# A decoder step on one core: the convolution state turned in another mixer, the sample rows of r finished in a step of their own, one order edge less

## The chip, the core and the metric

The kernel runs on one core of one Trainium2 chip, as one program. The time is device microseconds of that core. Five engines work side by side, each through its own instructions in order: TensorE (PE, with its weight loads shown as PEld), VectorE (DVE), ScalarE (ACT), GpSimd (POOL) and SyncE (SP), which here issues all the DMA transfers. The kernel before takes 2837.52 us (median of three runs, 2835.45 to 2838.09).

## The reference

One step of one layer of a hybrid decoder, in float32, for 2048 prompt tokens and, beside them, for 32 sample tokens (8 requests of 4). Cut to what matters here:

```python
def mixer(xn, s0, lp):
    q, k, v, r, a, u, sv = split_cols(xn @ w_in)
    ...
    o, S = gla_chunked(q, k, v, logg, s0)          # gated linear attention
    o = rmsnorm(o, g_gla_out).reshape(B, T, GLA_WIDTH) * jax.nn.silu(r)
    sv = rmsnorm(jax.nn.gelu(sv).reshape(B, T, SGU_HEADS, SGU_DH), g_sgu)
    z = sgu_spatial(sv, w_s, b_s)                  # mixing of positions in chunks of 128
    s_out = jax.nn.gelu(u) * z.reshape(B, T, SGU_WIDTH)
    return jnp.concatenate([o, s_out], axis=-1) @ w_out, S, sv

def conv_ffn(hn, buf, w_gate, w_up, conv_w, conv_b, w_down):
    g = hn @ w_gate
    gp = jnp.concatenate([buf, g], axis=1)         # buf: the last two rows, state_conv
    c = conv_b + sum(conv_w[j] * gp[:, j:j + T] for j in range(CONV_W))
    return (jax.nn.gelu(c) * (hn @ w_up)) @ w_down, gp[:, -2:]

def layer(x, mk, mv, s0, buf, ...):
    h = x + mixer(rmsnorm(x), s0)
    h = h + mem_attend(rmsnorm(h), mk, mv)         # attention over 256 memory tokens
    return h + conv_ffn(rmsnorm(h), buf)
```

## The kernel before

**Blocks.** The prompt is cut into four blocks of 512 tokens (`s` = 0 to 3). Each block goes through a mixer, the memory attention and the feed-forward network. I call the mixers of the four blocks mixer 1 to mixer 4. The 32 sample tokens ride along: in mixer 2 (`B.mix_sample`, s = 1) as 32 more columns, and in the feed-forward network of block 3 (`B.ffn_sample`, s = 2). In mixer 1, products of the memory's keys and values with weights are folded in between (`qk_steps`, `vo_steps`), whose tiles are `qkp` and `vop`.

**Matmuls.** A float32 product is made of three fast matmuls: each operand is split into a high part (an ACT copy) and a low part (a DVE subtraction); L99, L100 and L101 (`mm3`) are the three products. The splits of weights are L84 and L85. Plain float32 matmuls are used for small things.

**The projection of r.** `tm_steps` makes four steps per projection, each with two of the eight slices of the weight; the tiles `t_wr` collect 128 tokens each. For the sample tokens it works by another way: sixteen "spread" matmuls (L723) put partial sums of the 32 tokens into four groups of 32 rows, ACT copies them out (L727, tile `t_wr1t`), and one matmul with `sum4` (L747) adds the four groups. L887 is the Silu that takes the tiles of r out, four for the prompt's rows and one for the sample rows. The same function serves the projections of v and sv.

**What stands around it in mixer 2.** `mix(h)` (L927 for the prompt, tile `zp`; L935 for the samples, tile `zps`) mixes positions for one of four heads; then DVE (L930, L936), POOL (L940), ACT (`ch`, L84) and POOL again (`cl`) make of it one of the eight inputs `cat` of the output projection. The linear attention runs for two pairs of heads (`p` = 0, 1), each with `diag` (L1006 on POOL, L1009 on PE), seven `level` steps (L1035 to L1061, tiles `e` and `kr`, PE at L1057), `decay` (tiles `kh`, `ktp`, `km`), `states` (`kv`), `chunks` (`op`) and, for the samples, `smp`. Its tail normalizes rows (`onorm`, which reads r at L1187; `gate`, L1192) and turns them back (`back`, `otp`). The output projection `out_proj_steps` (tiles `a_wo`) begins with inputs 4 to 7, those of the mixes. In mixer 2 it has three first steps, `w1`.

**The convolution state.** `sample_conv` loads the sample tokens' convolution state in six pieces of 16 rows (L466, tiles `sc`), transposes it in 22 matmuls into one PSUM tile (L469, `sctp`) and copies that to `sct` (L470). POOL reads `sct` tile by tile for the network of block 3 (L1553), up to eight tiles ahead.

**What sets the order.** The program is a list of steps. `weave` places side lists between the main steps: a triple (steps, first, last) spreads the steps evenly from behind main step `first` to behind main step `last`. In mixer 2 the main steps are sv 0 to 3, a 4, k 5, q 6, v 7 to 10, u 11 and 12, r 13 to 16, then the output projection. Behind step 16 come mixes 3 and 4 and the last four steps of the linear attention; the tail is spread from 16 to 18. `run` loads weights five units ahead of their use. A planner then gives every instruction its place in its engine's order, by the order of the program, by its own model of time and by the buffers that are free: six T buffers (the tiles `e`, `kr`, `pr`, `z`, `sc`, `t_wr1t`, `y` and others), four PSUM banks for sums (`acc`) and four for everything small (`mps`). `behind(first, then)` adds an order edge without a wait: `then` may not stand before `first` on its engine. Two such edges bear on the output projection: in whole projections a matmul of its third row tile stands behind the last `op`; in mixer 2 its very first matmul stands behind the last matmul of the last mix (`B.last_mix`).

Of the kernel before, what the change touches and what calls it, by code (L numbers as in the profile page):

```python
# [12 lines left out]
AF = mybir.ActivationFunctionType  # L13
# [12 lines left out]
NS = 32  # L26
# [7 lines left out]
Q0, K0, V0, R0, A0, U0, SV0 = 0, 256, 512, 1024, 1536, 1552, 2064  # L34
# [3 lines left out]
def hymba_step_kernel(  # L38
# [10 lines left out]
    act, dve, pool, pe = nc.scalar, nc.vector, nc.gpsimd, nc.tensor  # L49
# [23 lines left out]
    def mps(name):  # L73
        return mmp.tile([128, 512], F32, tag="mm", name=name)
# [19 lines left out]
    def behind(first, then):  # L94

        tc.add_manual_dep(then.ins, first.ins.name, in_turn, reason="in turn")
# [270 lines left out]
    for l in range(7):  # L367
# [7 lines left out]
        m = const([128, 256], f"mask{l}", U8)  # L375
# [4 lines left out]
    sum4 = const([128, NS], "sum4")  # L380
# [96 lines left out]
    def weave(main, *sides):  # L477

        out = []
        due = [0.0] * len(sides)  # L480
        at = [0] * len(sides)
        for i, m in enumerate(main):
            out.append(m)
            for j, (steps, first, last) in enumerate(sides):
                if i < first:
                    continue
                due[j] = len(steps) * min(1.0, (i - first + 1) / (last - first + 1))
                while at[j] < len(steps) and at[j] < due[j] - 1e-9:
                    out.append(steps[at[j]])
                    at[j] += 1  # L490
        for j, (steps, _, _) in enumerate(sides):
            out += steps[at[j]:]
        return out
# [216 lines left out]
            return Step(fn, [wmake(w, 4 * j, 4, m0, 256, f"{name}{j}", make, j) for j in range(2)])  # L710
        return Step(fn, [(w, 4 * j, 4, m0, 256, f"{name}{j}") for j in range(2)])

    def tm_steps(w, m0, get_xs, sample, evac, name):


        ps = {}
        held = []

        def spread(j):
            if j == 1:  # L720
                ps["q"] = mps(f"t_{name}q")
            for k, raw in reversed(held):
                pe.matmul(ps["q"][hr[k % 4]], sxg[:, k * NS:(k + 1) * NS], raw, start=j == 1, stop=j == 3)  # L723
            held.clear()
            if j == 3:
                ps["t"] = T_(f"t_{name}t")
                act.activation(ps["t"][:, :512], ps["q"], AF.Copy)  # L727

        def fn(j, wu):
            xs = get_xs()  # L730
            raw, wh, wl = wu
            if sample:
                held.extend((2 * j + kk, raw[:, kk]) for kk in range(2))
                if j % 2:
                    spread(j)
            for c in range(4):
                cs = slice(c * 128, (c + 1) * 128)
                if j == 0:
                    ps[c] = acc(f"t_{name}{c}")
                for kk in range(2):  # L740
                    k = 2 * j + kk
                    mm3(ps[c], xs[k][0][:, cs], xs[k][1][:, cs], wh[:, kk], wl[:, kk], k == 0, k == 7)
                if j == 3:
                    evac(ps[c], c, 128)
            if sample and j == 3:
                ps[4] = mps(f"t_{name}4")
                pe.matmul(ps[4][:NS], sum4, ps["t"][:, :512], start=True, stop=True)  # L747
                evac(ps[4][:NS], 4, NS)

        def unit(j):  # L750
            def load():
                raw = wload(w, 2 * j, 2, m0, 512, f"{name}{j}")
                return raw, *wsplit(raw, f"{name}{j}")
            return load
        return [Step(lambda wu, j=j: fn(j, wu), [unit(j)]) for j in range(4)]

# [84 lines left out]
    def proj_steps(B):  # L843
        s, sample = B.s, B.mix_sample
        T = TM if sample else SB
        nt = 5 if sample else 4
        w = w_in[0]
        xs = lambda: B.xs

        def ev_tm(key, f):  # L850
            def evac(ps, c, n):
                if c == 0:
                    B.__dict__[key] = [U(f"{key}{s}{c}") for c in range(nt)]
                f(B.__dict__[key][c][:n, :512], ps, B.xrs[:n, c:c + 1])
            return evac

        def ev_fm(key, i0, f):
            def evac(mm, ps, c0, cw):
                i = i0 + mm
                if c0 == 0:  # L860
                    B.__dict__.setdefault(key, {})[i] = U(f"{key}{s}{i}")
                f(B.__dict__[key][i][:, c0:c0 + cw], ps, B.xbc[:, c0:c0 + cw])
            return evac

        scaled = lambda o, i, f: dve.tensor_scalar(o, i, f, None, ALU.mult)
        times = lambda o, i, f: dve.tensor_tensor(o, i, f, ALU.mult)

        def gelu_times(o, i, f):
            dve.tensor_tensor(o, i, f, ALU.mult)
            act.activation(o, o, AF.Gelu_apprx_tanh)  # L870

        def a_fn():
            B.aT = T_(f"aT{s}")
            for ci, (c0, cw) in enumerate(chunks_of(sample)):
                ps = mps(f"ap{s}{ci}")
                for k in range(8):
                    pe.matmul(ps[hr[k % 4], :cw], wa[:, k], B.h[k][:, c0:c0 + cw], start=k < 4, stop=k >= 4)
                act.activation(B.aT[:, c0:c0 + cw], ps[:, :cw], AF.Copy)

        out = tm_steps(w, SV0, xs, sample, ev_tm("sv", lambda o, i, f: act.activation(o, i, AF.Gelu_apprx_tanh, scale=f)), f"ws{s}")  # L880
        out.append(Step(a_fn))
        out.append(fm_step(w, K0, xs, sample, ev_fm("k", 0, times), f"wk{s}"))
        out.append(fm_step(w, Q0, xs, sample,
                           ev_fm("q", 0, lambda o, i, f: dve.scalar_tensor_tensor(o, i, 0.125, f, ALU.mult, ALU.mult)), f"wq{s}"))
        out += tm_steps(w, V0, xs, sample, ev_tm("v", scaled), f"wv{s}")
        out += [fm_step(w, U0 + h * 128, xs, sample, ev_fm("u", h, gelu_times), f"wu{s}{h}") for h in (0, 2)]
        out += tm_steps(w, R0, xs, sample, ev_tm("r", lambda o, i, f: act.activation(o, i, AF.Silu, scale=f)), f"wr{s}")  # L887
        return out

    def norm_of(src, ss, c, n):  # L890
# [59 lines left out]
    for p in range(2):  # L950
        t = cp.tile([128, 128], F32, tag=f"S{p}", name=f"Sz{p}", bufs=2)
# [270 lines left out]
    def out_proj_steps(B, unit, src, g, name, sample, first, finished, keep=None, seven=False,  # L1222
                       whole=False):
# [4 lines left out]
        s = B.s  # L1228
# [5 lines left out]
        def half(m2, k0, last, begin=True, end=True):  # L1234

            def fn(wu):
                wh, wl = wu
                x = src()
                if m2 == 0 and last:
                    B.hn, B.sq = [], None  # L1240
                for i in range(2):
                    m = 2 * m2 + i
                    ms = slice(i * 128, (i + 1) * 128)
                    for ci, (c0, cw) in enumerate(chunks_of(sample)):
                        cs = slice(c0, c0 + cw)
                        ps = acc(f"a_{name}{s}{k0}{m}{ci}") if begin else open_.pop(m)
                        for k in range(4):
                            mm = mm3(ps[:, :cw], wh[:, k, ms], wl[:, k, ms], x[k0 + k][0][:, cs], x[k0 + k][1][:, cs],
                                     begin and k == 0, end and k == 3)
                            if name == "wo" and s and not last and k == 0:  # L1250
                                if whole and m == 2:
                                    behind(B.last_o, mm)
                                elif not whole and m == ci == 0:
                                    behind(B.last_mix, mm)
                        if end:
                            dve.tensor_tensor(B.h[m][:, cs], ps[:, :cw], B.h[m][:, cs], ALU.add)
                        else:
                            open_[m] = ps
                    if last:
                        finish(m)  # L1260
            return Step(fn, [unit(k0, m2)])
# [35 lines left out]
        if whole:  # L1297
            out = [half(m2, first, False, end=False) for m2 in (0, 1)]
# [493 lines left out]
    for s, B in enumerate(blocks):  # L1792
# [6 lines left out]
        if B.mix_sample:  # L1799
            def keep():  # L1800
                if not hasattr(smp, "x"):
# [1 line left out]
                return smp.x  # L1803
        w1, w2, stat = out_proj_steps(B, lambda k0, m2, s=s: (w_out[0], k0, 4, m2 * 256, 256, f"wo{s}{k0}{m2}"),
                                      lambda B=B: B.cat, "gx", "wo", B.mix_sample, 4, B.mix_sample, keep, seven=True, whole=not B.mix_sample)
        early = [] if s else [Step(sample_conv)]
        folds = [(qk_steps, 0, 10), (vo_steps, 11, 19)] if s == 0 else []
        steps += weave(proj + w1, *folds, (after, 0, 5), (sgu_st[:1], 6, 6), (early, 9, 9), (sgu_st[1:nst], 11, 11), (sgu_st[nst:nst + 2], 12, 13), (sgu_st[nst + 2:], 16, 16), (gla[:1], 4, 4), (gla[1:2], 6, 6), (gla[2:12], 8, 10), (gla[12:-nlast], 10, 13), (gla[-nlast:], 16, 16), (gtail, 16, 18))
        scales, sc, turns = attention_steps(B)
        x1, x2, xstat = out_proj_steps(B, lambda k0, m2, s=s: wready(vod[k0 // 4][:, m2], f"wx{s}{k0}{m2}"),  # L1810
                                       lambda B=B: B.ao, "gffn", "wx", False, 0, B.ffn_sample, seven=s > 0, whole=True)
# [54 lines left out]
```

## Time and profile before

| | us |
|---|---|
| median of three runs | 2837.52 |
| profiled execution | 2838.75 |
| its span, first to last instruction | 2837.0 |
| PE busy | 2799.4 |
| DVE busy | 1892.2 |
| ACT busy | 1107.4 |
| POOL busy | 567.4 |

The mean granted clock of TensorE over the span is 0.994. How to read the rows: a timeline row gives the start, the time it took, the engine, the source line, the operation, the tile written and the tiles read, the shape and the count of merged instructions; in brackets stands how long the engine was idle before it and whose end it waited for. A row by stages gives, for a stretch of the span, the busy time of each engine with the number of its instructions, then the granted clock as a share of full speed. Matmuls overlap, so the spacing of their starts tells more than the time of one. A DMA row on SP is the issue of a transfer, not the transfer.

### The profile page before, as it was taken

The numbers are of one execution on the slowest core, as the hardware profiler recorded it, in microseconds if no ns is written. First come the engines' busy times: TensorE is split into PE (matmuls) and PEld (weight loads), VectorE is DVE, ScalarE is ACT, GpSimd is POOL, SyncE is SP. The second block draws the span as 40 slices with busy tenths as digits, with TensorE's granted clock in tenths as the row PEclk, the third lists the DMA queues.
The fourth block names the chain that finished last, engine by engine and source line by source line (L and its number), as shares of the span: only waits on it lengthen the run. The fifth ranks groups of instructions, "written<-read, shape, count | busy, mean of one in ns | idle before, by whom it ended". The sixth has DMA issues, their size and how long they took to land.

```text
span 2837.0 us, 47062 instructions
## 1 busy us (share of the span) xinstructions
PE 2799.4 (99%) x17894; PEld 2479.6 (87%) x17894; DVE 1892.2 (67%) x3266; ACT 1107.4 (39%) x1950; POOL 567.4 (20%) x638
## 2 busy tenths in 40 slices
PE   8999999999999999999999999999999999999998
PEld 8887888888887798998888889899999888899997
DVE  6577778777657686655545787666666688665555
ACT  5645545333363444322223545422223545431222
POOL 2002213111101221321321121232221013132222
PEclk9999999999999999999999999999999999999999
DMA  9755579999941236887886225576776324677775
GB/s 310 238 187 193 170 262 340 339 342 329 341 142 62 82 117 233 302 292 276 310 315 232 83 75 177 206 255 247 261 264 230 111 68 135 208 260 270 272 276 185
DMA packets 369687, 638.21 MB, mean 225 GB/s; under 512 B 27370, under 2 KB 238412, under 8 KB 369462
## 3 DMA queue, kind: packets, MB, share of 16 engines
q1 hardware_dynamic: 369462, 635.20, 65.7%
q8 instruction: 142, 2.33, 0.3%
q14 instruction: 83, 0.68, 0.1%
HBM read 507.69 MB, written 127.41 MB: 224 GB/s over the span
## 4 chain that ended last, share of the span: by engine, by line
PE 63%; DVE 3%; ACT 1%; DMA 0%; issue 0%; POOL 0%; DVEq 0%; ACTq 0%
PE d L101 4%; PE d L100 4%; PE d L99 4%; PE a_wx L101 2%; PE a_wx L100 2%; PE a_wx L99 2%; PE s L1057 1%; PE a_wo L99 1%; PE a_wo L100 1%; PE a_wo L101 1%; PE a_wu L99 1%; PE a_wu L100 1%; PE t_wr L99 1%; PE a_wu L101 1%; PE t_wr L100 1%; PE t_wr L101 1%
## 5 line engine op out<-in xcount | busy, mean ns | idle before, releaser
L99 PE MATMUL d<-acth,whi_wd 128*128 128x272 f32 (+1 forms) x688 | 235.3, 342 | 0.0
L100 PE MATMUL d<-actl,whi_wd 128*128 128x272 f32 (+1 forms) x688 | 233.8, 340 | 0.0
L101 PE MATMUL d<-acth,wlo_wd 128*128 128x272 f32 (+1 forms) x688 | 233.4, 340 | 0.0
L1714 DVE TENSOR_TENSOR h<-d,h 128x512 f32<-128x512 f32 (+1 forms) x232 | 133.7, 582 | 148.0 <-PE d L101 148.0
L1607 POOL TENSOR_TENSOR c<-c,bc_f 128x512 f32<-128x512 f32 (+1 forms) x88 | 138.0, 1574 | 135.7 <-ACT c L1606 135.0
L1597 ACT ACTIVATE c<-g,colsb 128x512 f32<-128x512 f32 x88 | 71.8, 816 | 189.4 <-DVE g L1560 142.0
L101 PEld LDWEIGHTS d<-acth,wlo_wd 128*128 128x128 f32 x688 | 129.3, 188 | 15.4 <-issue 1.2
L99 PEld LDWEIGHTS d<-acth,whi_wd 128*128 128x128 f32 x688 | 129.4, 188 | 13.8
L100 PEld LDWEIGHTS d<-actl,whi_wd 128*128 128x128 f32 x688 | 129.4, 188 | 13.7 <-issue 0.4
L1629 POOL TENSOR_TENSOR c<-r_q_wup,c 128x512 f32<-128x512 f32 (+1 forms) x33 | 63.4, 1922 | 332.4 <-DVE r_q_wup L296 212.4
L99 PE MATMUL a_wo<-ch,h_wo 128*128 128x512 f32 (+1 forms) x320 | 112.8, 366 | 2.6 <-ACT ch L88 2.1
L1594 POOL COPY carry<-g 128x2 f32<-128x2 f32 x88 | 29.9, 340 | 423.4 <-DVE g L1560 392.0
L100 PE MATMUL a_wo<-cl,h_wo 128*128 128x512 f32 (+1 forms) x320 | 113.6, 357 | 0.0
L101 PE MATMUL a_wo<-ch,l_wo 128*128 128x512 f32 (+1 forms) x320 | 112.5, 354 | 0.0
L1598 DVE SCALAR_TENSOR_TENSOR c<-g,colsb,c 128x512 f32<-128x512 f32 x88 | 85.4, 971 | 27.8 <-ACT c L1597 27.2
L101 PE MATMUL a_wx<-pTh,wlo_wx 128*128 128x512 f32 x256 | 101.2, 395 | 0.0
L100 PE MATMUL a_wx<-pTl,whi_wx 128*128 128x512 f32 x256 | 100.5, 393 | 0.0
L84 ACT ACTIVATE acth<-c 128x512 fp32r<-128x512 f32 (+1 forms) x88 | 55.9, 637 | 113.5 <-DVE c L1629 80.4
L99 PE MATMUL a_wx<-pTh,whi_wx 128*128 128x512 f32 x256 | 100.1, 394 | 0.0
L1606 ACT ACTIVATE c<-c 128x512 f32<-128x512 f32 (+1 forms) x88 | 56.1, 638 | 89.6 <-DVE c L1599 77.8
L1599 DVE SCALAR_TENSOR_TENSOR c<-g,colsb,c 128x512 f32<-128x512 f32 x88 | 88.4, 1004 | 1.1
L85 DVE TENSOR_TENSOR actl<-c,acth 128x512 fp32r<-128x512 f32 (+1 forms) x88 | 63.1, 719 | 26.7 <-ACT acth L84 25.6
(3753 smaller groups left out, 9731.8 us busy)
## 6 DMA issues: line engine op xcount, KB each, us to landing
whi_wd<-wd SPq DMA_DIRECT2D x66, 512.0 KB, 9.8
wlo_wd<-wd SPq DMA_DIRECT2D x66, 512.0 KB, 9.6
r_wo<-in_w_out_dram SPq DMA_DIRECT2D x32, 512.0 KB, 3.3
wlo_wx<-vod SPq DMA_DIRECT2D x32, 512.0 KB, 4.5
whi_wx<-vod SPq DMA_DIRECT2D x32, 512.0 KB, 4.1
r_wg<-in_w_gate_dram SPq DMA_DIRECT2D x22, 512.0 KB, 5.1
r_wup<-in_w_up_dram SPq DMA_DIRECT2D x22, 512.0 KB, 6.3
r_wd<-in_w_down_dram SPq DMA_DIRECT2D x22, 512.0 KB
```

What stands on the lines that cost most here:

```text
L84: act.activation(hi, src, AF.Copy)
L85: (lo_eng or dve).tensor_tensor(lo, src, hi.bitcast(F32), ALU.subtract)
L99: out = pe.matmul(ps, wh, xh, start=first, stop=False)
L100: pe.matmul(ps, wh, xl, start=False, stop=False)
L101: pe.matmul(ps, wl, xh, start=False, stop=last)
L1597: act.activation(c[:, :SB], g[:, 2:SB + 2], AF.Identity, bias=cb, scale=w2)
L1598: dve.scalar_tensor_tensor(c[:, :SB], g[:, 1:SB + 1], w1, c[:, :SB], ALU.mult, ALU.add)
L1599: dve.scalar_tensor_tensor(c[:, :SB], g[:, 0:SB], w0, c[:, :SB], ALU.mult, ALU.add)
L1606: act.activation(c[:, :T], c[:, :T], AF.Gelu_apprx_tanh)
L1607: pool.tensor_tensor(c[:, :T], c[:, :T], B.fbc[:, :T], ALU.mult)
L1629: (dve, pool)[i].tensor_tensor(c[:, :T], q[i], c[:, :T], ALU.mult)
L1714: dve.tensor_tensor(B.h[m + mm][:, cs], ps[:, :cw], B.h[m + mm][:, cs], ALU.add)
```

## The change

Three edits. First, `tm_steps` gets an argument `apart`. With it, the sum matmul of the sample rows and its Silu leave the fourth step and become a fifth step, `rows`, with an order edge that puts the matmul behind `apart()`. Only the projection of r in mixer 2 uses it, with the last matmul of the last mix. So mixer 2 has one main step more, number 17, and its tail is spread from 17 to 19, as before behind the step with the sample rows. In the program's order, mixes 3 and 4 and the last four steps of the linear attention now stand ahead of the sample rows of r. Second, the edge that put mixer 2's first matmul of the output projection behind the last mix is taken out; the edge of the whole projections stays. Third, `sample_conv` moves from behind main step 9 of mixer 1 to behind main step 1 of mixer 3. What is computed stays the same.

```diff
-    def tm_steps(w, m0, get_xs, sample, evac, name):
+    def tm_steps(w, m0, get_xs, sample, evac, name, apart=None):
...
-            if sample and j == 3:
-                ps[4] = mps(f"t_{name}4")
-                pe.matmul(ps[4][:NS], sum4, ps["t"][:, :512], start=True, stop=True)
-                evac(ps[4][:NS], 4, NS)
+            if sample and j == 3 and not apart:
+                rows()
+
+        def rows():
+            ps[4] = mps(f"t_{name}4")
+            mm = pe.matmul(ps[4][:NS], sum4, ps["t"][:, :512], start=True, stop=True)
+            if apart:
+                behind(apart(), mm)
+            evac(ps[4][:NS], 4, NS)
...
-        return [Step(lambda wu, j=j: fn(j, wu), [unit(j)]) for j in range(4)]
+        out = [Step(lambda wu, j=j: fn(j, wu), [unit(j)]) for j in range(4)]
+        return out + [Step(rows)] if apart else out
...
-        out += tm_steps(w, R0, xs, sample, ev_tm("r", ...), f"wr{s}")
+        out += tm_steps(w, R0, xs, sample, ev_tm("r", ...), f"wr{s}",
+                        (lambda: B.last_mix) if sample else None)
...
-                            if name == "wo" and s and not last and k == 0:
-                                if whole and m == 2:
-                                    behind(B.last_o, mm)
-                                elif not whole and m == ci == 0:
-                                    behind(B.last_mix, mm)
+                            if name == "wo" and s and whole and not last and (m, k) == (2, 0):
+                                behind(B.last_o, mm)
...
-        early = [] if s else [Step(sample_conv)]
+        early = [Step(sample_conv)] if B.ffn_sample else []
...
-        ... (early, 9, 9), ... (gtail, 16, 18))
+        ... (early, 1, 1), ... (gtail, 16 + B.mix_sample, 18 + B.mix_sample))
```

More of the change, by code (lines that the diff above doesn't have):

```diff
@@ L886, in proj_steps @@
         out += [fm_step(w, U0 + h * 128, xs, sample, ev_fm("u", h, gelu_times), f"wu{s}{h}") for h in (0, 2)]
-        out += tm_steps(w, R0, xs, sample, ev_tm("r", lambda o, i, f: act.activation(o, i, AF.Silu, scale=f)), f"wr{s}")
+        out += tm_steps(w, R0, xs, sample, ev_tm("r", lambda o, i, f: act.activation(o, i, AF.Silu, scale=f)), f"wr{s}",
+                        (lambda: B.last_mix) if sample else None)
         return out
@@ L1805, in hymba_step_kernel @@
                                       lambda B=B: B.cat, "gx", "wo", B.mix_sample, 4, B.mix_sample, keep, seven=True, whole=not B.mix_sample)
-        early = [] if s else [Step(sample_conv)]
+        early = [Step(sample_conv)] if B.ffn_sample else []
         folds = [(qk_steps, 0, 10), (vo_steps, 11, 19)] if s == 0 else []
-        steps += weave(proj + w1, *folds, (after, 0, 5), (sgu_st[:1], 6, 6), (early, 9, 9), (sgu_st[1:nst], 11, 11), (sgu_st[nst:nst + 2], 12, 13), (sgu_st[nst + 2:], 16, 16), (gla[:1], 4, 4), (gla[1:2], 6, 6), (gla[2:12], 8, 10), (gla[12:-nlast], 10, 13), (gla[-nlast:], 16, 16), (gtail, 16, 18))
+        steps += weave(proj + w1, *folds, (after, 0, 5), (sgu_st[:1], 6, 6), (early, 1, 1), (sgu_st[1:nst], 11, 11), (sgu_st[nst:nst + 2], 12, 13), (sgu_st[nst + 2:], 16, 16), (gla[:1], 4, 4), (gla[1:2], 6, 6), (gla[2:12], 8, 10), (gla[12:-nlast], 10, 13), (gla[-nlast:], 16, 16), (gtail, 16 + B.mix_sample, 18 + B.mix_sample))
         scales, sc, turns = attention_steps(B)
```

## The prediction

> **What bounds the kernel now.** I read, in this order, the page, the waits of TensorE (PE), PE's busy time and granted clock by stage, and the instruction timelines of PE, ACT, DVE, POOL and SP at the three places the change touches. From the page, then from PE's waits (engine, line, who ended it: us in all, times, longest):
>
> ```profile
> span 2837.0 us, 47062 instructions
> PE 2799.4 (99%) x17894; PEld 2479.6 (87%) x17894; DVE 1892.2 (67%) x3266; ACT 1107.4 (39%) x1950; POOL 567.4 (20%) x638
> ```
>
> ```profile
> PE s L1057 <- DVE kr L1047: 5.0, 2, 3.3
> PE t_wr L747 <- ACT t_wr1t L727: 3.6, 1, 3.6
> ```
>
> PE is busy for 2799.4 of 2837.0 us, so at most 37.6 us of idle time can be won, plus what a low clock costs; taking work from DVE, ACT, POOL or a queue is worth nothing unless PE waits for it. The second wait is that of the matmul which the change moves. The stages (from:to, length, busy us of PE, PEld, DVE, ACT, POOL, granted clock, DMA share, GB/s):
>
> ```profile
> 253.00:266.00 13.00, 10.02 (x32) 8.42 (x33) 8.95 (x16) 2.47 (x5) 1.72 (x1) 0.50 0.24 81
> 972.00:980.00 8.00, 8.00 (x32) 6.43 (x32) 1.66 (x3) 1.34 (x2) 1.34 (x1) 0.57 0.50 187
> 991.00:1011.00 20.00, 18.45 (x146) 16.54 (x146) 19.94 (x45) 5.35 (x7) 7.30 (x5) 0.98 0.27 80
> 1010.00:1017.00 7.00, 6.91 (x29) 6.14 (x30) 2.85 (x7) 2.13 (x5) 0.00 (x0) 0.51 0.67 185
> 1540.00:1560.00 20.00, 20.00 (x93) 16.22 (x92) 7.03 (x11) 7.09 (x12) 1.11 (x2) 1.00 0.48 150
> ```
>
> The first row lies in mixer 1: a stretch at half clock. The next three lie in mixer 2, which has two such stretches; in mixer 3, at 1540, PE is busy throughout at full clock. A microsecond of PE work therefore costs one in mixer 3, while mixers 1 and 2 hold idle time.
>
> **Part 1: sample rows of r, mixer 2.** PE there, with the idle time before an instruction and its releaser in brackets:
>
> ```profile
> 951.87 1.06 PE L927 MATMUL zp<-wsT,sv 128*128 128x128 f32 x8
> 952.86 0.40 PE L935 MATMUL zps<-wss,sv 32*128 32x32 f32 x2
> 953.19 0.50 PE L101 MATMUL t_wr<-h_wr,xl 128*128 128x512 f32 x1
> ...
> 966.43 1.93 PE L723 MATMUL t_wr1q<-r_wr,sxg 128*32 128x512 f32 x16
> 971.91 1.31 PE L747 MATMUL t_wr<-t_wr1t,sum 128*32 128x512 f32 x2 [3.56 <-ACT t_wr1t L727]
> 973.15 2.08 PE L927 MATMUL zp<-wsT,sv 128*128 128x128 f32 x8
> 975.15 0.63 PE L935 MATMUL zps<-wss,sv 32*128 32x32 f32 x2
> 975.72 2.08 PE L927 MATMUL zp<-wsT,sv 128*128 128x128 f32 x8
> ```
>
> ACT, then DVE:
>
> ```profile
> 968.95 2.42 ACT L887 ACTIVATE r<-t_wr,xrs 128x512 f32<-128x512 f32 x4
> 971.24 0.61 ACT L727 ACTIVATE t_wr1t<-t_wr1q 128x512 f32<-128x512 f32 x1
> ...
> 981.77 0.66 ACT L84 ACTIVATE ch<-z 128x544 fp32r<-128x544 f32 x1 [3.50 <-POOL z L940]
> ```
>
> ```profile
> 967.49 2.14 DVE L1105 TENSOR_SCALAR km<-ktps,blk 32x128 f32<-32x128 f32 x8
> 969.56 1.20 DVE L85 TENSOR_TENSOR l_wo<-r_wo,h_wo 128x1024 fp32r<-128x1024 f32 x1
> 975.26 0.75 DVE L930 SCALAR_TENSOR_TENSOR z<-zp,colsb,bsb 128x512 f32<-128x512 f32 x1 [4.50 <-PE zp L927]
> ...
> 1001.84 0.67 DVE L1187 TENSOR_TENSOR o<-o,r 32x512 f32<-32x512 f32 x1
> ```
>
> The spread matmuls end at 968.35 (971.91 − 3.56). Their copy, L727, stands on ACT behind four Silus and ends at 971.85, so L747 keeps PE idle for 3.56 us, and the mixes behind it with it. They need nothing of it. After the wait PE is slow: one mix with its sample part took 2.57 us (973.15 to 975.72), the same instructions 1.32 us before (951.87 to 953.19). From 972 to 980 the clock is 0.57, which loses 8.0 × 0.43 = 3.4 us. The place thus costs 3.56 + 3.4 = 7.0 us.
>
> Changed, the two mixes come first: 2 × 1.32 = 2.6 us at full clock, from 968.35 to 971.0. Their PSUM banks should be there: the last of the copies out of the p=1 transposes (km) ends at 969.63. L747 could then still wait 971.85 − 971.0 = 0.9 us at most, and nothing if matmuls of the output projection stand between; I take 0.4 us. Behind it on PE are only that projection and the state matmuls, work that is there either way. Its Silu moves along; the first reader of row tile 4 of r is L1187 at 1001.84, far behind. So 7.0 − 0.4 = **6.6 us** won, with ends of 7.0 and of about 4 (0.9 us waited, and 2 us of low clock left).
>
> [...]
>
> Does the gain reach the end of mixer 2? From 991 to 1011 DVE is busy 19.94 of 20 us, with norms that start from PE's o tiles. DVE is idle for 4.50 us behind l_wo, waiting for the zp of 973.15; that chain moves with PE, so I let the whole of it slide forward and the thin stretch of 1010 to 1017 with it.
>
> **Part 2: the edge.** Before, the projection's first matmul stands behind the last mix on PE; after, only L747 does. I cost this at nothing: every matmul freed is work that PE does anyway. What it costs if the planner uses the freedom badly is rival 3.
>
> **Part 3: the convolution state.** In mixer 1 (PE; DVE; POOL; all loads on SP with their times in ns to issue; PE later; DVE later):
>
> ```profile
> 173.75 0.40 PE L101 MATMUL t_wv<-h_wv,xl 128*128 128x512 f32 x1
> 173.98 0.40 PE L99 MATMUL t_wv<-h_wv,xh 128*128 128x512 f32 x1
> 174.31 1.55 PE L469 MATMUL sctp<-ident,sc 16*128 16x16 f32 x22
> 175.79 0.50 PE L100 MATMUL t_wv<-l_wv,xh 128*128 128x512 f32 x1
> ```
>
> ```profile
> 175.54 0.68 DVE L1035 TENSOR_TENSOR e<-b 128x512 f32<-128x512 f32 x1
> 176.13 0.52 DVE L470 COPY sct<-sctp 128x352 f32<-128x352 f32 x1
> ```
>
> ```profile
> 176.72 1.15 POOL L1553 COPY gs<-sct 128x16 f32<-128x16 f32 x8 [42.50 <-DVE sct L470]
> ```
>
> ```profile
> L466 SPq DMA_DIRECT2D sc<-in_state_conv_dram x6: 389/462/663, 153.7 to 171.6; - x6
> ```
>
> ```profile
> 169.20 1.05 PE L1057 MATMUL s<-kr,e 128*128 128x128 f32 x8
> ...
> 253.33 2.05 PE L1057 MATMUL s<-kr,e 128*128 128x128 f32 x8 [3.31 <-DVE kr L1047]
> ```
>
> ```profile
> 226.84 0.75 DVE L930 SCALAR_TENSOR_TENSOR z<-zp,colsb,bsb 128x512 f32<-128x512 f32 x1 [1.13 <-PE zp L927]
> ```
>
> The 22 transposes put 175.79 − 173.98 = 1.81 us between two matmuls that otherwise follow at 0.23 us: 1.58 us of PE. With them go one DVE copy (0.52 us), six loads on SP (0.39 to 0.66 us each to issue) and eight POOL copies that ran right behind.
>
> In mixer 3 PE has no gap: **+1.58 us**; DVE (7.03 of 20 us) and POOL (1.11) have room. On SP the loads cost at most 6 × 0.66 = 4 us of issue among weight loads that run five units ahead; on POOL the copies stand ahead of the row norms' powers (L316), 1.15 us, and hold these back if the state comes late. Bounds: the row's own 1.55 us, and, if PE reaches the transposes before the loads have landed, a stall like that of Part 1, 7 us more.
>
> In mixer 1 PE comes 1.58 us earlier to its wait at 250.0 (253.33 − 3.31). It gains only if the level chain it waits for comes earlier too. That chain's last leg starts on DVE behind the z of 226.84, which itself waited for PE (1.13 us). So it moves by the same 1.58 us: **−1.58 us**, the two cancel. Bounds: nothing won, if DVE paces the chain further back; or the whole stall gone: 5.0 us of waits for kr and 13.0 × 0.50 = 6.5 us of low clock, 11.5 us.
>
> **Sum.** 0 − 6.6 + 1.6 − 1.6 = −6.6 us. The profiled execution took 2838.75 us (span 2837.0, 1.75 around it): 2832.2. The median of the runs, 2837.52, is 1.2 us below it: **2831 us**.
>
> **Rivals.**
> 1. *Mixer 1 loosens.* The six state tiles share six T buffers with the levels. A level's e was written only at 175.54, right after the first state tiles were read (174.31); the level before had been used by 170.3 (169.20 + 1.05). Without the tiles the chain could be up to 175.54 − 170.3 = 5.3 us ahead, more than the first wait of 3.31 us, so that the clock stays up. Against it: DVE is crowded later, and the chain is released by PE at 226.8. Worth 3.3 to 11.5 us; middle 7.4: 2824 us.
> 2. *The gain is given back.* The norms at 991 to 1011 fill DVE; if something other than PE starts them, PE waits for them longer by what it came earlier, and 1010 to 1017 keeps its low clock. For it: DVE's 19.94 of 20. Against it: DVE's idle time before 991. 2837 us.
> 3. *Slower: PE takes the projection first.* Without the edge its first matmuls, whose inputs come from mixes 1 and 2, can go ahead of the mixes of heads 3 and 4; PE executes in order, then meets the inputs of the last two heads and waits. The way from the last zp (975.72) to its ch (982.43) is 6.7 us at present. If the fill is used up by then, PE idles 6.7 us, loses 3.4 us by the clock, and DVE's norms start later by the 3.0 us of projection put first (four banks, two inputs, three matmuls of 18.45 / 146 = 0.126 us): 13.1 instead of 7.0 us, so 2843.6 us. [...] Against it: the state matmuls (16 kv, then op) still fill.
> 4. *No effect*: the planner may keep L747 where PE waits for ACT (another ACT instruction put ahead of L727), 2837.5 us.
>
> **How the numbers follow.** A measurement of this kernel tells 0.2% (5.7 us) from no change. Forecast 0.48, by itself 2828 to 2835; rival 1 0.22, rival 2 0.12, rival 3 0.13, rival 4 0.05. Of the forecast's chance 0.30 lies beyond 5.7 us (below 2831.8) and 0.18 within. Faster: 0.30 + 0.22 = 0.52. Same: 0.18 + 0.12 + 0.05 = 0.35. Slower: 0.13. The range 2820 to 2840 leaves out the strongest form of rival 1 and rival 3's upper half and beyond, and takes in a late load in mixer 3.
>
> **What would show it.** Right: no idle time before L747 over 1 us; the two zp groups near 968 to 971 at 1.06 us each; clock 1.00 from 966 to 985; 22 transposes of 1.5 us in mixer 3 without a wait; mixer 1's end moved by about 1.6 us. Wrong: PE idle before a_wo or zp in mixer 2 for over 3 us (rival 3), the thin stretch before 1017 grown (rival 2), or the waits for kr at 250 us gone (rival 1) or longer.

## The result, and the profile after

The changed kernel takes 2824.78 us (median of six runs, 2822.55 to 2829.24) where the kernel before took 2838.69 us beside it (six runs, 2835.45 to 2840.13): a ratio of 0.9953, 95% interval 0.9941 to 0.9966, so 9.7 to 16.7 us of 2838.7, middle 13.3. Repeated later (label a_again below): 0.9957, 0.9945 to 0.9968. The forecast was 2831.0 us, its range 2820 to 2840. The whole interval lies beyond the 0.2% that tell from no change; the direction holds, and the gain is twice the 6.6 us forecast.

From the page of the changed kernel, and from its waits of PE (engine, tile, line, who ended the wait: us in all, times, longest), behind two longer ones at the program's start (2.9 and 2.4 us):

```profile
span 2827.5 us, 47048 instructions
PE 2795.2 (99%) x17894; PEld 2475.8 (88%) x17894; DVE 1887.1 (67%) x3266; ACT 1105.9 (39%) x1950; POOL 572.6 (20%) x638
```

```profile
PE otp L1205 <- DVE vol L85: 2.2, 2, 1.3
PE mkt L588 <- DVE mkf L579: 2.0, 1, 2.0
PE ktp L1103 <- POOL kh L1100: 1.8, 1, 1.8
PE a_wk L99 <- ACT sv L886: 1.3, 1, 1.3
```

The two waits that headed the list before, 5.0 us for `kr` and 3.6 us for `t_wr1t`, are gone. PE idles 2827.5 − 2795.2 = 32.3 us instead of 37.6. The rest of the 9.5 us between the two profiled spans (the changed kernel's profile is of its slowest run, 2829.24 us) is clock: adding up length × (1 − granted clock) over the whole span in 283 equal stretches gives 17.4 us lost before and 11.3 us after. 5.3 + 6.1 = 11.4 us, less 1.9 us by which PE's work itself came out longer.

Mixer 2, PE of the changed kernel (start, time, engine, line, tiles, shape, count):

```profile
960.62 1.92 PE L723 MATMUL t_wr1q<-r_wr,sxg 128*32 128x512 f32 x16
962.48 1.16 PE L934 MATMUL zp<-wsT,sv 128*128 128x128 f32 x8
...
963.90 0.39 PE L99 MATMUL a_wo<-ch,h_wo 128*128 128x272 f32 x1
...
966.25 1.06 PE L934 MATMUL zp<-wsT,sv 128*128 128x128 f32 x8
...
968.40 1.09 PE L1122 MATMUL kv<-v,kt 128*64 128x128 f32 x16
...
980.43 1.02 PE L750 MATMUL t_wr<-t_wr1t,sum 128*32 128x512 f32 x2
```

The mixes follow the spread matmuls at once. Matmuls of the output projection (`a_wo`) already stand between the two mixes, which the edge forbade before. The sum matmul (now L750) starts 980.43 − 966.03 = 14.4 us after ACT has ended the copy that it reads (L727, 965.41 to 966.03) and waits for nothing.

Mixer 1, PE of the kernel before (its `s` of 253.33, with the wait of 3.31 us, stands in the prediction), then of the changed kernel:

```profile
237.77 1.05 PE L1057 MATMUL s<-kr,e 128*128 128x128 f32 x8
...
245.97 1.06 PE L927 MATMUL zp<-wsT,sv 128*128 128x128 f32 x8
...
257.11 2.05 PE L1057 MATMUL s<-kr,e 128*128 128x128 f32 x8 [1.73 <-DVE kr L1047]
260.08 1.11 PE L1096 MATMUL ktp<-ident,kh 128*128 128x128 f32 x4 [0.93 <-POOL kh L1093]
```

```profile
172.14 1.05 PE L1064 MATMUL s<-kr,e 128*128 128x128 f32 x8
...
233.80 1.05 PE L1064 MATMUL s<-kr,e 128*128 128x128 f32 x8
...
242.24 1.06 PE L934 MATMUL zp<-wsT,sv 128*128 128x128 f32 x8
251.04 1.05 PE L1064 MATMUL s<-kr,e 128*128 128x128 f32 x8
252.42 1.13 PE L1064 MATMUL s<-kr,e 128*128 128x128 f32 x8 [0.33 <-ACT h_wof L84]
255.38 1.11 PE L1103 MATMUL ktp<-ident,kh 128*128 128x128 f32 x4 [1.83 <-POOL kh L1100]
```

The level matmuls (`s`, 237.77 to 233.80) and the mix (`zp`, 245.97 to 242.24) stand 3.97 and 3.73 us earlier, not 1.58. The true shift is larger still: the profiled execution of the changed kernel was 2.94 us behind when it came here (the `s` at 169.20 in the prediction stands at 172.14), so counted from that `s` it is 6.91 and 6.67 us. Before, 253.33 − 245.97 − 3.31 = 4.05 us of PE work lay between `zp` and the next `s`, and then PE waited. After, 251.04 − 242.24 = 8.80 us of work lie there and no wait follows. The way from the start of `zp` to the end of the `kr` that this `s` needs did not get shorter: 252.32 + 0.87 − 245.97 = 7.22 us before, 247.51 + 1.91 − 242.24 = 7.18 us after. So 4.05 us of work could not cover it, and 8.80 us can. On DVE, the `kr` for the earlier `s`, of 237.77 before and 233.80 after, moved by less than that `s`. The kernel before, then the changed kernel, each with both `kr`:

```profile
233.60 0.88 DVE L1047 SCALAR_TENSOR_TENSOR kr<-e,sel,q 128x256 f32<-128x256 f32 x2
...
252.32 0.87 DVE L1047 SCALAR_TENSOR_TENSOR kr<-e,sel,q 128x256 f32<-128x256 f32 x2
```

```profile
232.11 0.87 DVE L1054 SCALAR_TENSOR_TENSOR kr<-e,sel,q 128x256 f32<-128x256 f32 x2
...
247.51 1.91 DVE L1054 SCALAR_TENSOR_TENSOR kr<-e,sel,q 128x256 f32<-128x256 f32 x2
```

The inputs of that `s` came 1.49 us earlier (233.60 to 232.11), but PE took it 3.97 us earlier (237.77 to 233.80): 2.5 us of weight matmuls that PE did ahead of it before now stand behind it, as filling for the later wait.

Stages of mixer 1, of the kernel before and then of the changed one (from:to, length, busy us of PE, PEld, DVE, ACT, POOL, granted clock, DMA share, GB/s):

```profile
253.00:268.00 15.00, 12.02 (x41) 10.01 (x42) 9.79 (x18) 4.20 (x8) 1.72 (x1) 0.57 0.31 103
282.00:308.00 26.00, 22.94 (x111) 18.50 (x110) 17.75 (x30) 10.34 (x15) 5.82 (x4) 0.93 0.58 192
```

```profile
253.00:268.00 15.00, 13.17 (x64) 11.18 (x64) 11.68 (x17) 8.11 (x12) 2.21 (x2) 0.89 0.65 210
282.00:308.00 26.00, 23.21 (x99) 18.35 (x99) 17.20 (x29) 10.79 (x17) 5.67 (x4) 0.87 0.51 164
```

Around 250 the kernel before lost 3.31 + 1.73 + 0.93 us of waiting and 15 × 0.43 = 6.45 us of clock, 12.4 us; the changed one 0.33 + 1.83 and 15 × 0.11 = 1.65, 3.8 us. That is 8.6 us. Of it, 1.6 us are given back in mixer 1's tail in these two executions, where the clock is 0.87 instead of 0.93 over 26 us. With the 1.58 us of transposes that are gone this makes 8.6 us, and the traces agree: from the `s` named above to the spread matmuls of mixer 2 it takes 966.43 − 169.20 = 797.23 us before and 960.62 − 172.14 = 788.48 us after, 8.75 us less.

Mixer 3, PE of the changed kernel:

```profile
1547.18 0.40 PE L101 MATMUL t_ws<-h_ws,xl 128*128 128x512 f32 x1
1547.51 0.66 PE L469 MATMUL sctp<-ident,sc 16*128 16x16 f32 x8
1548.10 0.50 PE L99 MATMUL t_ws<-h_ws,xh 128*128 128x512 f32 x1
1548.53 1.04 PE L469 MATMUL sctp<-ident,sc 16*128 16x16 f32 x14
1549.50 0.50 PE L100 MATMUL t_ws<-l_ws,xh 128*128 128x512 f32 x1
1549.83 0.39 PE L101 MATMUL t_ws<-h_ws,xl 128*128 128x512 f32 x1
```

PE doesn't wait. The transposes are split in two groups and take 1549.83 − 1547.18 − 3 × 0.23 = 1.96 us more than the three steps of 0.23 us alone (the expectations below have 1.95). POOL's copies behind them wait for the state, but POOL's next power (L316) waits 3.69 us for DVE after them anyway.

### The profile page after: what moved, and what is told of

It reads as the page before. It is cut to its first block, busy times and chain, and to the rows that moved or that the text cites. A ratio compares the mean times of both kernels' runs of the same rounds, so it can differ in the third digit from the quotient of the medians.

```text
span 2827.5 us, 47048 instructions
## 1 busy us (share of the span) xinstructions
PE 2795.2 (99%) x17894; PEld 2475.8 (88%) x17894; DVE 1887.1 (67%) x3266; ACT 1105.9 (39%) x1950; POOL 572.6 (20%) x638
## 4 chain that ended last, share of the span: by engine, by line
PE 65%; DVE 2%; DMA 0%; ACT 0%; issue 0%; POOL 0%; SPq 0%; DVEq 0%; ACTq 0%
PE d L99 4%; PE d L101 4%; PE d L100 4%; PE a_wx L99 2%; PE a_wx L101 2%; PE a_wx L100 2%; PE a_wo L99 1%; PE a_wo L100 1%; PE a_wo L101 1%; PE s L1064 1%; PE t_wr L101 1%; PE t_wr L99 1%; PE t_wr L100 1%; PE a_wu L99 1%; PE a_wu L100 1%; PE a_wu L101 1%
## 5 line engine op out<-in xcount | busy, mean ns | idle before, releaser
L1603 DVE SCALAR_TENSOR_TENSOR c<-g,colsb,c 128x512 f32<-128x512 f32 x88 | 88.4, 1004 | 1.1
```

The lines of the kernel that those rows point to most:

```text
L1603: dve.scalar_tensor_tensor(c[:, :SB], g[:, 0:SB], w0, c[:, :SB], ALU.mult, ALU.add)
```

## Experiments

"Before" is the kernel before, "changed" the changed kernel. A ratio is always to runs of the kernel before on the same chip.

**The two halves of the change.** First the rows of r and the edge alone; the convolution state stays in mixer 1:

```diff
-        early = [Step(sample_conv)] if B.ffn_sample else []
+        early = [] if s else [Step(sample_conv)]
...
-        ... (early, 1, 1) ...
+        ... (early, 9, 9) ...
```

> Parts 1 and 2 alone (the sample rows of r in a step of their own, the edge out); the convolution state stays in mixer 1. Theory A, the wait and the low clock behind it are the gain: the 3.56 us wait for ACT's copy is gone, the clock is 1.00 from 966 to 985, and the time falls by 6 to 9 us (ratio about 0.9975). Theory B, the whole gain comes from mixer 1 because its order changed: no change here, within 2 us of before. Theory C, the edits help only together: less than 3 us.

Measured: 2830.55 us, ratio 0.9974 (0.9965 to 0.9982), so 7.4 us won (5.1 to 9.9). Then the convolution state alone: before, with the two lines of the change that move it.

> Part 3 alone: the convolution state in mixer 3, everything else as before. As the prediction summed it (1.58 us less in mixer 1, 1.58 us more in mixer 3): no change within 1.5 us, mixer 1's waits at about 250 us as long as before. As its first rival has it (the six state tiles held the T buffers of the level chain): the waits for kr near 250 us shrink from 5.0 us to under 1 us, the stretch at half clock behind them with them, and the time falls by 4 to 9 us. If the effects are local to each mixer, this and the run of parts 1 and 2 alone add up to the 13.9 us of the whole change.

Measured: 2835.41 us, ratio 0.9987 (0.9978 to 0.9996), so 3.7 us won (1.1 to 6.2), a little under the 4 to 9 us that its expectation gave for rival 1, though the waits for `kr` went as it said. 0.9974 × 0.9987 = 0.9961, within the interval of the whole: the two parts add up. From PE's waits, the first half alone and then the second half alone:

```profile
PE s L1064 <- DVE kr L1054: 5.0, 2, 3.3
```

```profile
PE t_wr L747 <- ACT t_wr1t L727: 3.7, 1, 3.7
```

Each half leaves the other's wait where it was. In the first half alone the wait for `t_wr1t` is gone, in the second that for `kr`, but for 0.24 us. So the rows of r are worth what was forecast for them, and the convolution state, forecast at nothing, is worth the rest. The first half also starts mixer 2's tail one step later (17 to 19); that was not tested by itself.

**The edge.** The changed kernel with the edge put back:

```diff
-                            if name == "wo" and s and whole and not last and (m, k) == (2, 0):
-                                behind(B.last_o, mm)
+                            if name == "wo" and s and not last and k == 0:
+                                if whole and m == 2:
+                                    behind(B.last_o, mm)
+                                elif not whole and m == ci == 0:
+                                    behind(B.last_mix, mm)
```

> The changed kernel with the edge put back (the projection's first matmul behind the last mix). As the prediction has it, the edge is worth nothing: the same time as the changed kernel within 1 us, ratio to before about 0.9953. If the projection matmuls between the two last mixes matter as filling for PE: up to 2 us slower than the changed kernel. If they hold the mixes up: up to 2 us faster.

Measured: 2826.72 us, ratio 0.9962 (0.995 to 0.9975), against 0.9953 and 0.9957 for the changed kernel. The edge makes no difference that can be measured; with these intervals that means less than some 4 us either way, so the 2 us that the expectation asked about stay undecided.

**What holds mixer 1's chain: the work, or the buffers?** The kernel before, in which the six state tiles stay where they are in the program but take buffers of another pool, so that the six T buffers are left to the levels:

```diff
-            t = T_(f"sc{j}")
+            t = U(f"sc{j}")
```

> The kernel before, with the six state tiles of mixer 1 in the pool of 49 U buffers instead of the six T buffers; nothing is moved. If T buffers held the level chain back, the chain's e of level 2 starts some 6 us or more earlier than 175.5 us, mixer 1's waits at 250 us shrink, and the time falls by 4 to 9 us although the transposes stay in mixer 1. If the gain in mixer 1 comes from taking 1.58 us of transposes off PE there, or only from the move: no change within 1.5 us.

Measured: 2839.84 us, ratio 1.0005 (0.9996 to 1.0014): no change. PE, in order of time, and a stage:

```profile
179.64 0.39 PE L469 MATMUL sctp<-ident,sc 16*128 16x16 f32 x4 [3.51 <-DMA sc<-in_state_conv_dram]
...
248.23 1.06 PE L927 MATMUL zp<-wsT,sv 128*128 128x128 f32 x8
257.03 1.05 PE L1057 MATMUL s<-kr,e 128*128 128x128 f32 x8
258.42 1.13 PE L1057 MATMUL s<-kr,e 128*128 128x128 f32 x8 [0.33 <-ACT h_wof L84]
```

```profile
180.00:188.00 8.00, 8.00 (x47) 7.49 (x47) 7.93 (x16) 0.72 (x2) 2.31 (x7) 0.57 0.21 69
```

The order around 250 is now that of the changed kernel: 257.03 − 248.23 = 8.80 us of work between `zp` and `s`, and no wait for `kr`. The 22 transposes are still there. The level's `e` that the prediction's rival 1 pointed at, written at 175.54 before, comes over 20 us earlier in both kernels without the state tiles in the T buffers (DVE; this one, then the changed kernel):

```profile
152.36 0.69 DVE L1035 TENSOR_TENSOR e<-b 128x512 f32<-128x512 f32 x1
```

```profile
154.70 0.68 DVE L1042 TENSOR_TENSOR e<-b 128x512 f32<-128x512 f32 x1
```

So it is the T buffers that the state tiles held, and not the 1.58 us of PE work, that kept the chain late. The other traces agree: PE has 4.04 to 4.05 us of work between `zp` and `s` in the three kernels whose state tiles sit in T buffers in mixer 1 (before, the first half alone, and the copy on DVE below), and 8.79 to 8.81 us in all the others but one, whose folds were moved (the second attempt below, 6.16 us). But the loads, too, are issued at another time (173.3 to 175.7 instead of 153.7 to 171.6), and PE now waits 3.51 us for them and loses 8 × 0.43 = 3.4 us of clock behind that: 6.9 us, most of the gain at 250. The time alone would have said that the buffers don't matter. That the new order is worth time by itself rests on the other runs, not on this one, whose profiled execution (2834.92 us) was moreover 4.9 us below its median.

**What mixer 1 wins and what mixer 3 pays.** Both kernels with the convolution state left out (zeros from POOL in its place): the kernel before, then the changed one.

```diff
     def sample_conv():
-        scd = state_conv[0].rearrange("b t f -> (b t) f")
...
-        dve.tensor_copy(sct.rearrange("p f t -> p (f t)"), sctp[:, :FT * 16])
+        pool.memset(sct.rearrange("p f t -> p (f t)"), 0.0)
```

> The kernel before with the convolution state left out altogether: no loads, no transposes, no copy; POOL fills the tile sct with zeros instead, so the sample tokens' part of the convolution that comes from the state is wrong. What mixer 1 alone gains by the move is read from this. My theory: the gain is the move's 3.7 us plus what mixer 3 pays for it, 1.95 us by its profile, so about 5.6 us: 2832.7 us, ratio 0.998. Rival 'they cancel' (the prediction's own step): only the 1.58 us of PE work goes, 2836.7 us, ratio 0.9994. Rival 'the gain is larger and mixer 3 pays more than its profile row': 8 us or more, 2830 us or less, ratio 0.997 or less. The waits for kr at 250 us are gone by my theory and by the last, and there by the first rival.

> The changed kernel with the convolution state left out in the same way (zeros instead of loads, transposes and copy). What mixer 3 pays is read from this. My theory: 1.95 us, so 2.0 us below the changed kernel's 2824.8: about 2822.8 us, ratio to before 0.9946 to 0.995. Rival 'mixer 3 pays more than its row' (loads on SP or copies on POOL that hold something else back): 4 us or more, 2821 us or less, ratio 0.994 or less. Rival 'nothing' (PE had room): 2824.8 us.

Measured: before without the state 2831.28 us, ratio 0.997 (0.9958 to 0.9981), so 8.5 us less (5.4 to 11.9); changed without the state 2826.0 us, ratio 0.9958 (0.9944 to 0.9971), where the changed kernel itself had 0.9953 and 0.9957. The first refutes "they cancel" (1.58 us) and agrees with the rows: 8.6 us around 250, less 1.6 given back, plus 1.58 of work that is gone, 8.6 us. It was more than the 5.6 us that I expected, though its interval still holds 5.6. The second gives no cost at all in mixer 3, within about 5 us either way, while 8.5 − 3.7 from the other pair gives 4.8 us, with intervals of some 3 us each. The times don't fix it closer, but the traces do. Between the two powers on POOL (L316) that stand around the transposes, 14.55 to 14.56 us pass in the five traces with the state in mixer 3, and 12.57 to 12.62 us in the seven without it: 1.9 to 2.0 us, as the row says. What mixer 1 wins is read in the same way, from the first `e` of its levels to the spread matmuls of mixer 2: 819.3 and 819.4 us before and in the first half alone, 808.3 to 811.1 us in the changed kernel (both profiles), the second half alone, with the edge back, without the state (both) and in the first attempt below. That is 8 to 11 us. (It is 816.2 us in the second attempt, 818.1 with the state in the other pool and 822.2 with the copy on DVE.) Less 1.9 us it is more than the 3.7 us (1.1 to 6.2) measured for the second half alone; where that run lost the rest, isn't known.

**Another engine for the copy.** Before, with the copy of L727 on DVE for r, instead of reordering:

```diff
-                act.activation(ps["t"][:, :512], ps["q"], AF.Copy)
+                if name[:2] == "wr":
+                    dve.tensor_copy(ps["t"][:, :512], ps["q"])
+                else:
+                    act.activation(ps["t"][:, :512], ps["q"], AF.Copy)
```

> The kernel before, with one edit: for r, the copy of the sample rows' partial sums (L727) runs on DVE instead of ACT. The sum matmul keeps its place in front of the mixes. If ACT's queue (four Silus ahead of the copy) is what PE waits for, the wait of 3.56 us falls below 2 us, the stretch at half clock behind it goes or shrinks, and the time falls by 3 to 8 us, as much as parts 1 and 2 alone (ratio 0.9974). If the mixes' early start is what counts, less than 2 us.

Measured: 2839.64 us, ratio 1.0008 (1.0 to 1.0017). PE's wait and the stage around it:

```profile
PE t_wr L750 <- DVE t_wr1t L728: 3.1, 1, 3.1
```

```profile
974.00:982.00 8.00, 5.08 (x32) 3.89 (x33) 4.55 (x11) 4.14 (x7) 1.36 (x1) 1.00 0.95 327
```

I had expected a wait under 2 us. PE waits 3.06 us for DVE's copy, almost as long as the 3.56 us for ACT's; what held the copy back on DVE isn't in these rows. What helped here is that PE has other work ahead of the sum (7.4 us won in the first half alone), not which engine copies. The clock stayed at 1.00 here behind 3.1 us of waiting, and the time still didn't fall. In this execution PE idled 2837.3 − 2796.1 = 41.2 us in all, 3.6 us more than before, though less at this place; where and why wasn't followed.

**The changed kernel again.** It is the same program as the changed kernel, to see what differs between two profiled executions.

> The changed kernel once more, beside the next ones on one chip. It should repeat its ratio of 0.9953 (0.9941 to 0.9966). Its profile is a second look at the same order of instructions: if stretches at half clock follow from the waits alone, they stand where they stood, behind the waits of 1.3 us at 108 us and of 1.8 us at 255 us; if it also hangs on when the wait falls, a stretch behind a wait of 1 to 2 us is there in one profile and missing in the other, while none is missing behind waits of over 3 us.

Measured: 2824.85 us (2819.31 to 2830.87), ratio 0.9957. Stages, the first profile of the changed kernel (253 to 268 stands above) and then this one:

```profile
104.00:116.00 12.00, 9.80 (x56) 7.19 (x57) 2.35 (x3) 10.59 (x31) 0.00 (x0) 0.86 0.77 263
...
286.00:300.00 14.00, 11.21 (x43) 8.41 (x42) 9.63 (x15) 5.20 (x9) 2.70 (x2) 0.76 0.74 242
```

```profile
104.00:116.00 12.00, 10.62 (x68) 7.85 (x67) 3.57 (x7) 9.44 (x28) 0.00 (x0) 1.00 0.87 304
253.00:268.00 15.00, 13.17 (x70) 11.14 (x70) 12.44 (x18) 9.58 (x14) 3.82 (x3) 1.00 0.73 243
286.00:300.00 14.00, 11.21 (x43) 8.46 (x42) 8.03 (x13) 4.49 (x8) 1.91 (x1) 0.76 0.64 219
```

From 253 to 268 PE idles the same 15 − 13.17 = 1.83 us in both, and the clock falls behind it in one and not in the other.

**Two attempts at a better version.** Both start from the changed kernel. In the first the convolution state is loaded and turned ahead of mixer 1, during the projection of the memory's keys, in buffers of the other pool:

```diff
-            t = T_(f"sc{j}")
+            t = U(f"sc{j}")
...
-    steps += weave(mem_steps, (norm, 0, 11), ([Step(late_constants)], 2, 2))
+    steps += weave(mem_steps, (norm, 0, 11), ([Step(sample_conv)], 1, 1), ([Step(late_constants)], 2, 2))
...
-        early = [Step(sample_conv)] if B.ffn_sample else []
+        early = []
```

> The changed kernel, but with the convolution state loaded and turned while the memory's keys are projected, ahead of mixer 1, in U buffers. If the six T buffers it held in mixer 1 are the whole reason for the gain there, mixer 1 keeps the changed kernel's order and its short waits at 250 us, and mixer 3 is relieved of the 1.95 us: 0 to 3 us faster than the changed kernel. If the gain in mixer 1 needs the state in mixer 3, it is slower than the changed kernel by 3 us or more.

Measured: 2827.4 us, ratio 0.9968 (0.9956 to 0.998): not better than the changed kernel. Two of PE's waits, both at the start:

```profile
PE mkt L588 <- DVE mkf L579: 3.2, 1, 3.2
...
PE colpsb L402 <- DMA rowsb<-in_conv_b_dram: 2.4, 1, 2.4
```

The first was 2.0 us in the changed kernel (1.4 in the kernel before), the second is new: the work has moved into another thin place. In the second attempt the folds of the memory's values (`vop`) end at main step 17 of mixer 1 instead of 19:

```diff
-        folds = [(qk_steps, 0, 10), (vo_steps, 11, 19)] if s == 0 else []
+        folds = [(qk_steps, 0, 10), (vo_steps, 11, 17)] if s == 0 else []
```

> The changed kernel, with the folds of values and output weights in mixer 1 spread up to main step 17 instead of 19, so that they are over before the tail's transposes. If the waits of these transposes for DVE's low parts of the folds (2.2 us near 291 us, with a stretch at half clock behind them in the changed kernel's profile) are worth their waits and clock, it is 2 to 6 us faster than the changed kernel; if the folds are needed there as filling for PE, it is slower.

Measured: 2835.01 us, ratio 0.9991 (0.9982 to 1.0), about 10 us slower than the changed kernel. Waits of its mixer 1:

```profile
PE otp L1205 <- DVE o L1199: 3.9, 3, 2.4
...
PE s L1064 <- DVE kr L1054: 2.4, 2, 1.2
PE ktp L1103 <- POOL kh L1100: 2.3, 1, 2.3
```

These come to 8.6 us. In the changed kernel the waits at these places were 4.5 us (2.2 for `vol` and 0.4 for `o` in the tail, 1.8 for `kh`, none for `kr`). The folds filled waits there; taken out, they left PE 4.1 us more without work, of which 2.4 us are waits for `kr` that are back. The rest of the 10 us is not in these rows. No version beat the changed kernel.

## Why the prediction was right, and where it wasn't

**Part 1, right.** Forecast 6.6 us with ends of 7.0 and about 4; measured 7.4 us (5.1 to 9.9). The sum matmul waits for nothing, so the 0.4 us left over for it wasn't needed. The 2 us of low clock in the lower end were my estimate; the traces don't show them: from 966 to 985 the clock is 1.00 in the first half alone and in the changed kernel. The second mix runs at 1.06 us and the first at 1.16, where the slow ones before took 2.08.

**The tail of mixer 2 slides, right.** The first half alone kept the gain, so rival 2 (all of it given back between 991 and 1017) is refuted. The low stretch of 1010 to 1017, which lost 7.00 × 0.49 = 3.4 us before, is one of 2 × (0.18 + 0.50 + 0.17) = 1.7 us from 998 to 1004 in the changed kernel.

**Part 2, right.** No gain or cost of the edge was measured, to within some 4 us. Rival 3 expected PE to run into the inputs of the last two heads without it; the projection's matmuls did go ahead, between the mixes, but the state matmuls (`kv` at 968.40) filled PE behind them, as the prediction's own counter-argument had it.

**Part 3, mixer 3, nearly right.** Forecast 1.58 us without a wait; its row gives 1.96 us, with the transposes cut in two groups, and the twelve traces give 1.9 to 2.0. No row shows a cost on POOL.

**Part 3, mixer 1, wrong.** The step that failed is "So it moves by the same 1.58 us: −1.58 us, the two cancel". I had followed the chain back to one release, the `z` of 226.84 on DVE, and taken the order of instructions on PE as given. The order did not stay. That `z` stands at 224.91 in the changed kernel; counted from the `s` of 169.20 and 172.14 that is 1.93 + 2.94 = 4.87 us earlier, three times the 1.58. PE took the later level matmuls and the mix earlier by 6.9 and 6.7 us, counted in the same way, and kept 8.80 us of work, not 4.05, to do between `zp` and `s`. With the state tiles out of the T buffers this order appears even where all their work stays. This is rival 1, "mixer 1 loosens", with the buffers that it named. Its 5.3 us of lead was too small: it took the level's `e` to be bound by the use of the level before, at 170.3, and without the tiles that `e` is written at 152.4 to 154.7. It had priced the gain at 3.3 to 11.5 us, middle 7.4; measured, 8.5 us for mixer 1 and 3.7 us for the whole move. Its bound "the whole stall gone, 11.5 us" wasn't reached, since 1.83 us of waiting for `kh` came up behind the waits for `kr`, and with the clock that is 3.8 us left.

So the time, 2824.8 us, came out near rival 1's 2824 and not at the forecast's 2831; the range held because it had been drawn wide enough for most of rival 1. Rival 1 was no alternative to Part 1: its 2824 is the forecast less 7.4 us, so it already adds both gains, and both happened. How near it came is partly luck, since 7.4 us was the middle of a wide range and the two halves measured alone give 7.4 + 3.7 = 11.1 us. Why the planner's order turns on the T buffers was seen in the orders of the kernels, not inside the planner, and stays open.

**The clock.** I priced one low stretch from its row at 3.4 us. The profiles here show stretches that lost 3.4 us and 1.7 us (last section), so half of my price was possible too. What sets the sizes in the traces (1.7, 3.4, 5.1 and 6.8 us), and where such a stretch begins, no run here shows.

## What to carry to other kernels

A side task's cost isn't only its own work: look which buffers it holds while it waits its turn, and test that alone, by giving it buffers of its own, and with the profile beside the time, since the freed wait and a new one can cancel. When a planner sets the order, don't carry a chain forward with the old order of the engine that bounds it; ask how much filling would stand ahead of each wait. Two outcomes that can both happen aren't rivals: give their sum a time and a chance of its own, and ask of each what it does to the other.

## What the runs showed of the hardware

**In these traces low clock cost about 1.7 us or a multiple of it.** Length × (1 − clock), from the rows above and in the prediction: 12 × 0.14 = 1.7 and 15 × 0.11 = 1.65 us once each in the changed kernel; 14 × 0.24 = 3.4 us in its tail of mixer 1; 8.0 × 0.43 = 3.4 us before, behind the wait in mixer 2, and the same 3.4 us behind the new wait for the loads; 15 × 0.43 = 6.45 us before at 253. They are close to one, two and four times 1.7; taken over its whole length, 252 to 266, the last comes to 6.8. In stretches of 2 us over all twelve traces, every such place but the one at the very end of the program lost 1.7, 3.4, 5.1 or 6.8 us.

**The length of a wait did not decide by itself whether the clock fell.** Behind 3.31 us (before, 0.50 from 253 to 266), 3.51 us (the state in the other pool, 0.57 from 180 to 188) and 3.56 us (before, 0.57 from 972 to 980) it fell. Behind 3.06 us it once did not (the copy on DVE, 1.00 from 974 to 982). Behind 1.83 us it fell in one execution of the changed kernel (0.89 from 253 to 268) and not in another (1.00). Nor was the loss the same: behind the waits of 3.31, 1.73 and 0.93 us at 250 it was 6.8 us before, and 5.1 us behind the same waits in the kernel with the copy on DVE. This fits much of the spread between runs, though it is not shown to be all of it: the changed kernel ran from 2822.55 us at a mean clock of 0.999 to 2829.24 us at 0.996, and 0.003 of 2827 us is 8.5 us, but two of its later runs at 0.997 still lie 4.4 us apart (2826.47 and 2830.87). A difference of 3 us can't be read off one profiled execution of this kernel; the half with the convolution state alone was profiled at 2829.13 us while its median was 2835.41.
